# A fixed order for three layer norms: scale and shift of a channel chunk one step ahead, and later places for the transpositions of the later chunks

## The chip, the cores and the metric

The kernel runs on one core of a Trainium2 chip. The metric is the device time of one execution, in microseconds (us). Its engines work side by side and each takes its instructions in the order written for it: TensorE (PE, with its weight loads shown apart as PEld), VectorE (DVE), ScalarE (ACT), GpSimd (POOL), and SyncE (SP), which issues the transfers.

## The reference

Two decoder layers over 256 positions of 2048 channels. What matters here is the frame around the mixers:

```python
for layer in range(DEPTH):                       # DEPTH = 2
    mix = even_mixer(...) if layer % 2 == 0 else odd_mixer(...)
    h = layer_norm(DEEPNORM_ALPHA * h + mix, ln_g[layer, 0], ln_b[layer, 0])
    ffn = conv_ffn(h, ffn_w_up[layer], ...)      # (silu(conv(x@up_a)) * (x@up_u)) @ w_down
    h = layer_norm(DEEPNORM_ALPHA * h + ffn, ln_g[layer, 1], ln_b[layer, 1])
```

So there are four layer norms. Each ends a matrix product whose result it needs whole (mean and variance run over all 2048 channels), and the product that follows each of the first three needs its output. All is float32.

## The kernel before, in words

**Products.** A float32 number is split into a high part `hi` and a rest `lo`, both in a format that TensorE multiplies, and a product is made of three: hi with hi, hi with lo, lo with hi. Weights come from memory in slabs: SP issues the load of a slab into one of four buffers `wraw` (L102), ACT writes `whi` (L108), DVE writes `wlo` (L109), each again into one of four buffers. The call that does these three for the next slab is named "pump". Nearly all of the kernel is a stream of such slabs with matmuls behind it.

**What sets the order.** The products are emitted one after another; a scheduler that knows the dependencies sets the order on the engines. Between the two marks `strict_from` and `strict_to`, which lie around each norm, every engine but SP keeps exactly the order in which the program wrote its instructions. SP's transfers are placed by the scheduler.

**A norm.** Tokens come in two halves, t = 0 and t = 1, of 128 each, on the partitions; `r` holds the 2048 channels as four chunks c = 0 to 3 of 512. For the last column group of the product before the norm, the matmuls of half 0 end first and those of half 1 are held back (the stretch "t1"), to give the norm of half 0 something to hide behind. Then, for each half and chunk (two digits, "12" is half 1, chunk 2):

- `first` and `second` on DVE (L226, L230): subtract the mean and multiply by the gain, then multiply by the inverse deviation and add the bias. Both work on `r` in place; `shift` is the two of them. Gains and biases lie in tiles borrowed from the feed-forward part (`tmp`, `c`, `u`, `row`, `fpad`), by their chunk.
- `turn`: four transpositions of 128x128 on TensorE (L255) into a PSUM tile `ps`, then ACT copies them to the `hi` part of `x` (L256).
- `lo` on DVE (L261): the rest, into the `lo` part of `x`.

`x` holds 16 k-tiles (128 channels each), so a chunk is four of them.

**The head of the next product.** While the norm runs, TensorE starts on the next product with the k-tiles that are there already; the first weight slabs for it lie ready in a place of their own. In the norms 0 and 2 (the feed-forward product follows) the head has eight k-tiles and three passes, `h0` (half 0), `h1` (half 1) and `lo` (the lo parts of the weights), done in `head_b` (L341 and L348); its stream goes on in `group_b` (L317). In norm 1 (the odd mixer's input product follows) the head has four k-tiles and two passes `h0` and `h1`, done in `head_a`, and `group_a` goes on from k-tile 4 (places "on"); all its matmuls stand on L356 to L358. After each k-tile the program calls `turns.at(place, k)`, and the table `plan` of the class `Norm` says which steps are written there. Norm 3 ends the kernel and has no such table.

At the pumps of the table the slabs behind the head are prepared: slabs 8 to 11 in the norms 0 and 2, slabs 4 to 7 in norm 1.

Of the kernel before, what the change touches and what calls it, by code (L numbers as in the profile page):

```python
# [80 lines left out]
class Weights:  # L81


    def __init__(self, tc, pool, streams):
        self.tc, self.nc, self.pool, self.slabs, self.done = tc, tc.nc, pool, [], 0
        at = {k: 0 for k in streams}
        self.first = []
        for src, kind, parts, nk in jobs():
            width = sum(n for _, n in parts)
            self.first.append(len(self.slabs))  # L90
            for m in slab_sizes(kind, nk):
                self.slabs.append((streams[src], at[src], kind, m, width))
                at[src] += 128 * m * width
        self.ready = {}
        self.limit = len(self.slabs)
# [64 lines left out]
class Norm:  # L160


    def __init__(self, trunk, idx, stats):
        self.k, self.idx, self.stats = trunk, idx, stats
        small = trunk.small
        self.mv = small.tile([128, 2, 2], F32, name="mv", bufs=2)
        self.rs = small.tile([128, 2, 2], F32, name="rs", bufs=2)
        self.plan = {}
        if idx == 3:
            x = trunk.keep.tile([128, 2, DM], F32, name="x")  # L170
            self.gb = [[x[:, i, 512 * c:512 * c + 512] for i in range(2)] for c in range(4)]
        else:
            self.gb = trunk.row_tiles()
            p = "fill", 0, 0
            self.plan = {("t1", 5): ["turn00", "lo00"], ("t1", 7): ["turn01"], ("norm", 0): ["first00", "first01", "second00", "second01"],
                         ("norm", 1): ["lo01", "shift10", "shift11"]}
            if idx == 1:
                more = {("h0", 2): ["turn10", "lo10"], ("h1", 0): ["pump", "turn11", "lo11"],
                        ("h1", 1): ["pump", "shift02", "turn02", "lo02"],
                        ("h1", 2): ["pump", "shift12", "turn12", "lo12"],  # L180
                        ("h1", 3): ["shift03", "pump", "shift13"], ("on", 5): ["turn03", "lo03"],
                        ("on", 7): ["turn13", "lo13"]}
            else:
                more = {("h0", 5): ["turn10", "lo10"], ("h0", 7): ["turn11", "lo11"],
                        ("h1", 3): ["shift02", "turn02", "lo02", "pump"],
                        ("h1", 6): ["shift12", "turn12", "lo12", "pump"],
                        ("lo", 1): ["shift03", "turn03", "lo03", "pump"],
                        ("lo", 4): ["shift13", "turn13", "lo13", "pump"]}
            self.plan.update(more)
        gb = trunk.I["gb"]  # L190
        for c in range(4):
            for i in range(2):
                trunk.nc.sync.dma_start(self.gb[c][i], bass.AP(
                    tensor=gb.tensor, offset=gb.offset + 4096 * idx + 2048 * i + 512 * c, ap=[[0, 128], [1, 512]]))
        self.ps = {}
# [1074 lines left out]
```

## Time and profile before

| | |
|---|---|
| time, median of 3 runs | 2329.18 us (2328.76 to 2329.88) |
| the profiled execution's own time | 2331.47 us |
| its span, first to last instruction | 2329.7 us |
| mean granted TensorE clock over the span | 0.996 |
| busy: PE, DVE, ACT | 2300.9, 1420.1, 1105.4 us |
| norm 0, from its first turn to the end of its head | 376.5 to 406.4 us |
| norm 1, the same | 1119.1 to 1142.8 us |
| norm 2, the same | 1576.4 to 1604.9 us |

Times in a timeline count from the first instruction of the span. A row of the timeline gives start, duration, engine, line and operation, what it writes and reads, how often (rows that follow one another at once are merged), and in brackets the idle time of the engine before it with what ended it. Matmuls overlap, so the distance of two starts says more than a duration.

### The profile page before, as it was taken

The page shows a single profiled execution, that of the slowest core. Times are in us where ns is not written, and L with a number is a line of the kernel's source. Part 1 is how long each engine was busy: PE and PEld are TensorE (multiplying, and loading weights), DVE is VectorE, ACT ScalarE, POOL GpSimd, SP SyncE. Part 2 cuts the span into 40 slices and gives each one's busy share as a digit, 9 for nine tenths or more (in the row PEclk, how much of TensorE's full clock was granted, in tenths as well). Part 3 has the DMA queues.
Part 4 walks back from the last instruction along what each step waited for, and adds up shares of the span by engine and source line. Part 5 has one row for each costly group of instructions (what it writes and reads, how often), then busy time and mean ns, then how long its engine had stood idle before and what let it go on. Part 6 is the DMA issues. An engine that isn't in the chain of part 4 may idle for free.

```text
span 2329.7 us, 32013 instructions
## 1 busy us (share of the span) xinstructions
PE 2300.9 (99%) x12550; PEld 1986.0 (85%) x12550; DVE 1420.1 (61%) x1921; ACT 1105.4 (47%) x1429; POOL 20.5 (1%) x32
## 2 busy tenths in 40 slices
PE   9999999999999999999999999999999999999998
PEld 9888888888888888888789888888888888888886
DVE  5677666666666664445645667766666666654445
ACT  5554542555555554334345554444555555543332
POOL 0001000000000000000000000000000000000000
PEclk9999999999999999999999999999999999999999
DMA  8664474666666667667456734583666666676664
GB/s 284 192 192 148 161 239 126 192 189 189 185 190 189 190 197 215 196 192 224 146 165 213 222 104 140 164 275 108 192 190 186 188 190 188 189 223 198 194 191 143
DMA packets 128248, 436.63 MB, mean 187 GB/s; under 512 B 14256, under 2 KB 16992, under 8 KB 127712
## 3 DMA queue, kind: packets, MB, share of 16 engines
q1 hardware_dynamic: 128096, 434.58, 60.5%
q8 instruction: 98, 1.61, 0.3%
q14 instruction: 54, 0.44, 0.1%
HBM read 432.41 MB, written 2.11 MB: 187 GB/s over the span
## 4 chain that ended last, share of the span: by engine, by line
PE 96%; DVE 1%; DMA 1%; ACT 0%; issue 0%; SPq 0%; POOL 0%; DVEq 0%; ACTq 0%; POOLq 0%
PE acc L317 57%; PE acc L356 10%; PE acc L358 10%; PE acc L357 10%; PE ps L358 1%; PE ps L356 1%; PE ps L357 1%; PE ps L676 1%; DMA wraw<-in_ev_in 1%; PE ps L255 1%; DVE wlo L109 1%; PE acc L341 0%; PE ps L317 0%; PE ps L615 0%; ACT whi L108 0%; DVE r L230 0%
## 5 line engine op out<-in xcount | busy, mean ns | idle before, releaser
L109 DVE TENSOR_TENSOR wlo<-wraw,whi 128x1024 fp32r<-128x1024 f32 (+4 forms) x794 | 950.0, 1198 | 640.8 <-ACT whi L108 639.4
L317 PE MATMUL acc<-x,whi 128*128 128x512 f32 x3776 | 1178.3, 397 | 0.0
L108 ACT ACTIVATE whi<-wraw 128x1024 fp32r<-128x1024 f32 (+4 forms) x794 | 822.9, 1037 | 732.8 <-PE acc L358 290.2
L317 PEld LDWEIGHTS acc<-x,wlo 128*128 128x128 f32 x3776 | 692.4, 188 | 156.6 <-issue 0.2
L317 PE MATMUL acc<-x,wlo 128*128 128x256 f32 x3776 | 726.1, 279 | 0.0
L317 PEld LDWEIGHTS acc<-x,whi 128*128 128x128 f32 x3776 | 584.2, 189 | 12.5 <-issue 1.2
L356 PE MATMUL acc<-whi,A 128*128 128x512 f32 x448 | 175.9, 393 | 0.0
L358 PE MATMUL acc<-whi,A 128*128 128x512 f32 x448 | 174.5, 390 | 0.0
L357 PE MATMUL acc<-wlo,A 128*128 128x512 f32 x448 | 174.5, 390 | 0.0
L408 ACT ACTIVATE tmp<-acc 128x512 f32<-128x512 f32 x120 | 71.6, 597 | 215.9 <-PE acc L317 213.8
L356 PE MATMUL acc<-whi,B 128*128 128x512 f32 x388 | 150.9, 389 | 0.0
L357 PE MATMUL acc<-wlo,B 128*128 128x512 f32 x388 | 150.9, 389 | 0.0
L358 PE MATMUL acc<-whi,B 128*128 128x512 f32 x388 | 150.9, 389 | 0.0
L358 PEld LDWEIGHTS acc<-whi,A 128*128 128x128 f32 x448 | 84.1, 188 | 17.7 <-DVE A L277 0.3
L356 PEld LDWEIGHTS acc<-whi,A 128*128 128x128 f32 x448 | 84.1, 188 | 17.3 <-ACT A L276 0.4
L357 PEld LDWEIGHTS acc<-wlo,A 128*128 128x128 f32 x448 | 84.2, 188 | 17.0
L356 PE MATMUL acc<-whi,x 128*128 128x512 f32 (+4 forms) x272 | 93.3, 344 | 0.3 <-ACT V L697 0.3
L357 PE MATMUL acc<-wlo,x 128*128 128x512 f32 (+4 forms) x272 | 92.9, 342 | 0.0
L358 PE MATMUL acc<-whi,x 128*128 128x512 f32 (+4 forms) x272 | 92.8, 341 | 0.0
L356 PEld LDWEIGHTS acc<-whi,B 128*128 128x128 f32 x388 | 72.8, 188 | 15.2
L357 PEld LDWEIGHTS acc<-wlo,B 128*128 128x128 f32 x388 | 72.8, 188 | 15.1
L358 PEld LDWEIGHTS acc<-whi,B 128*128 128x128 f32 x388 | 72.8, 188 | 15.1
(289 smaller groups left out, 1630.6 us busy)
## 6 DMA issues: line engine op xcount, KB each, us to landing
wraw<-in_up SPq DMA_DIRECT2D x328, 512.0 KB, 3.9
wraw<-in_down SPq DMA_DIRECT2D x176, 512.0 KB, 4.2
wraw<-in_od_in SPq DMA_DIRECT2D x96, 512.0 KB, 4.1
wraw<-in_ev_in SPq DMA_DIRECT2D x72, 512.0 KB, 3.6
wraw<-in_ev_out SPq DMA_DIRECT2D x32, 512.0 KB, 4.1
wraw<-in_od_out SPq DMA_DIRECT2D x32, 512.0 KB, 4.4
wraw<-in_up SPq DMA_DIRECT2D x32, 384.0 KB, 3.5
wraw<-in_ev_in SPq DMA_DIRECT2D x16, 348.0 KB, 4.5
```

What stands on the lines that cost most here:

```text
L108: nc.scalar.activation(hi[:, :n], raw[:, :n], AF.Copy)
L109: nc.vector.tensor_tensor(lo[:, :n], raw[:, :n], hi[:, :n].bitcast(F32), op=OP.subtract)
L255: nc.tensor.transpose(ps[:, 128 * i:128 * i + 128], T.r[:, t, 512 * c + 128 * i:512 * c + 128 * i + 128], T.ident)
L317: nc.tensor.matmul(acc, wt, mv, start=(k == 0 and i < len(unit)), stop=(k == nk - 1 and i >= len(unit)))
L356: nc.tensor.matmul(o, xh, wh, start=first, stop=False)
L357: nc.tensor.matmul(o, xh, wl, start=False, stop=False)
L358: nc.tensor.matmul(o, xl, wh, start=False, stop=last)
L408: nc.scalar.activation(t, a[:, :, 256:], AF.Copy, scale=sign)
L676: nc.tensor.matmul(o[:, t * 128:(t + 1) * 128], a, b, start=(i == 0), stop=(i == len(mms) - 1))
```

## The change

Only the table `plan` is changed, for the norms 0 to 2. No instruction is added, taken away or altered. The lines behind the table stand three lines higher afterwards (L255 is L252, L226 is L223, L230 is L227, L261 is L258, L915 is L912).

```diff
             if idx == 1:
-                more = {("h0", 2): ["turn10", "lo10"], ("h1", 0): ["pump", "turn11", "lo11"],
-                        ("h1", 1): ["pump", "shift02", "turn02", "lo02"],
-                        ("h1", 2): ["pump", "shift12", "turn12", "lo12"],
-                        ("h1", 3): ["shift03", "pump", "shift13"], ("on", 5): ["turn03", "lo03"],
-                        ("on", 7): ["turn13", "lo13"]}
+                more = {("h0", 2): ["turn10", "lo10", "shift02"], ("h1", 0): ["turn11", "lo11", "shift12", "pump"],
+                        ("h1", 1): ["turn02", "lo02", "shift03", "pump"],
+                        ("h1", 2): ["turn12", "lo12", "shift13", "pump"], ("h1", 3): ["pump"],
+                        ("on", 5): ["turn03", "lo03"], ("on", 7): ["turn13", "lo13"]}
             else:
-                more = {("h0", 5): ["turn10", "lo10"], ("h0", 7): ["turn11", "lo11"],
-                        ("h1", 3): ["shift02", "turn02", "lo02", "pump"],
-                        ("h1", 6): ["shift12", "turn12", "lo12", "pump"],
-                        ("lo", 1): ["shift03", "turn03", "lo03", "pump"],
-                        ("lo", 4): ["shift13", "turn13", "lo13", "pump"]}
+                more = {("h0", 5): ["turn10", "lo10"], ("h0", 7): ["turn11", "lo11", "shift02", "shift12"],
+                        ("h1", 4): ["turn02", "lo02", "pump"], ("h1", 7): ["turn12", "shift03", "lo12", "pump"],
+                        ("lo", 3): ["turn03", "shift13", "lo03", "pump"], ("lo", 6): ["turn13", "lo13", "pump"]}
```

DVE in norm 0, from the step lo10 on, before. L261 is `lo`, L226 and L230 are `first` and `second` (tile `u` and `row`: chunk 2; `fpad`: chunk 3), L109 is the DVE part of a pump.

```order
L261 TENSOR_TENSOR x<-ps,x 128x4x128 x2
L226 SCALAR_TENSOR_TENSOR r<-r,mv,u 128x512
L230 SCALAR_TENSOR_TENSOR r<-r,rs,row 128x512
L261 TENSOR_TENSOR x<-ps,x 128x4x128
L109 TENSOR_TENSOR wlo<-wraw,whi 128x768
L226 SCALAR_TENSOR_TENSOR r<-r,mv,u 128x512
L230 SCALAR_TENSOR_TENSOR r<-r,rs,row 128x512
L261 TENSOR_TENSOR x<-ps,x 128x4x128
L109 TENSOR_TENSOR wlo<-wraw,whi 128x768
L226 SCALAR_TENSOR_TENSOR r<-r,mv,fpad_3392 128x512
L230 SCALAR_TENSOR_TENSOR r<-r,rs,fpad_3393 128x512
```

The same place after the change:

```order
L258 TENSOR_TENSOR x<-ps,x 128x4x128 x2
L223 SCALAR_TENSOR_TENSOR r<-r,mv,u 128x512
L227 SCALAR_TENSOR_TENSOR r<-r,rs,row 128x512
L223 SCALAR_TENSOR_TENSOR r<-r,mv,u 128x512
L227 SCALAR_TENSOR_TENSOR r<-r,rs,row 128x512
L258 TENSOR_TENSOR x<-ps,x 128x4x128
L109 TENSOR_TENSOR wlo<-wraw,whi 128x768
L223 SCALAR_TENSOR_TENSOR r<-r,mv,fpad_3392 128x512
L227 SCALAR_TENSOR_TENSOR r<-r,rs,fpad_3393 128x512
L258 TENSOR_TENSOR x<-ps,x 128x4x128
L109 TENSOR_TENSOR wlo<-wraw,whi 128x768
```

The scale and shift of 12 now stands ahead of the `lo` of 02 and its pump, and that of 03 ahead of the `lo` of 12. Norm 2 has the same rows.

DVE in norm 1, from lo10 on, before. `A<-prm` writes a small piece for the odd mixer into the area `A`, which holds the head's weight slabs until TensorE is done with them.

```order
L261 TENSOR_TENSOR x<-ps,x 128x4x128
L109 TENSOR_TENSOR wlo<-wraw,whi 128x1024
L261 TENSOR_TENSOR x<-ps,x 128x4x128
L109 TENSOR_TENSOR wlo<-wraw,whi 128x1024
L226 SCALAR_TENSOR_TENSOR r<-r,mv,u 128x512
L230 SCALAR_TENSOR_TENSOR r<-r,rs,row 128x512
L261 TENSOR_TENSOR x<-ps,x 128x4x128
L109 TENSOR_TENSOR wlo<-wraw,whi 128x1024
L226 SCALAR_TENSOR_TENSOR r<-r,mv,u 128x512
L230 SCALAR_TENSOR_TENSOR r<-r,rs,row 128x512
L261 TENSOR_TENSOR x<-ps,x 128x4x128
L226 SCALAR_TENSOR_TENSOR r<-r,mv,fpad_9188 128x512
```

The same place after the change, down to the last `second`:

```order
L223 SCALAR_TENSOR_TENSOR r<-r,mv,u 128x512
L227 SCALAR_TENSOR_TENSOR r<-r,rs,row 128x512
L109 TENSOR_TENSOR wlo<-wraw,whi 128x1024
L258 TENSOR_TENSOR x<-ps,x 128x4x128
L223 SCALAR_TENSOR_TENSOR r<-r,mv,fpad_9188 128x512
L227 SCALAR_TENSOR_TENSOR r<-r,rs,fpad_9189 128x512
L109 TENSOR_TENSOR wlo<-wraw,whi 128x1024
L258 TENSOR_TENSOR x<-ps,x 128x4x128
L223 SCALAR_TENSOR_TENSOR r<-r,mv,fpad_9188 128x512
L274 TENSOR_TENSOR A<-prm,A 128x16x2 x2
L227 SCALAR_TENSOR_TENSOR r<-r,rs,fpad_9189 128x512
L109 TENSOR_TENSOR wlo<-wraw,whi 128x1024 x3
```

The `shift` of 02 has gone ahead of lo11 (it stands above the first of these rows), that of 12 ahead of the first pump; each pump comes one step later, and the wlo of the slabs 6 and 7 stand behind the last `shift`.

SP in norm 1, before and then after: slabs 4 to 11 of the odd input product, the small loads `row` and `cs` for the odd mixer, further slabs, `dec` (1 MB).

```order
L102 DMA wraw<-in_od_in 128x1024 x8
L915 DMA row<-in_c_row 128x1
L967 DMA cs<-in_c_rot 128x512
L102 DMA wraw<-in_od_in 128x1024
L968 DMA dec<-in_c_decay 128x2048
L102 DMA wraw<-in_od_in 128x1024 x19
```

```order
L102 DMA wraw<-in_od_in 128x1024 x6
L912 DMA row<-in_c_row 128x1
L964 DMA cs<-in_c_rot 128x512
L102 DMA wraw<-in_od_in 128x1024 x5
L965 DMA dec<-in_c_decay 128x2048
L102 DMA wraw<-in_od_in 128x1024 x17
```

The loads `row` and `cs` are issued two slabs earlier, ahead of the slabs 10 and 11, and `dec` two slabs later.

## The prediction

> **What bounds the kernel now.** I read the page's busy times first, then TensorE's own waits, then the timeline of the engines around each norm, and last the stretches with their granted clock.
>
> ```profile
> PE 2300.9 (99%) x12550; PEld 1986.0 (85%) x12550; DVE 1420.1 (61%) x1921; ACT 1105.4 (47%) x1429; POOL 20.5 (1%) x32
> PE ps L255 <- DVE r L230: 15.8, 8, 3.1
> PE ps L255 <- DVE r L230: 5.4, 3, 1.8
> PE ps L255 <- DVE r L230: 4.9, 2, 3.1
> ```
>
> TensorE is the bound, with DVE and ACT far behind. The waits (total us, times, longest) name one cause that matters: the transposition (L255) waits for `second` (L230), 15.8 us in eight waits, over half of the 2329.7 - 2300.9 = 28.8 us that TensorE is idle at all. The last two rows are the same question for the stretches of norm 0 and norm 1; norm 2 answers like norm 0. So all a better order can win is here, plus what a stop drags behind it. DVE in norm 0 shows why the shift is late:
>
> ```profile
> 386.24 0.69 DVE L261 TENSOR_TENSOR x<-ps,x 128x512 fp32r<-128x512 f32 x1 [1.17 <-ACT x L256]
> 386.85 0.74 DVE L226 SCALAR_TENSOR_TENSOR r<-r,mv,u 128x512 f32<-128x512 f32 x1
> 387.63 0.75 DVE L230 SCALAR_TENSOR_TENSOR r<-r,rs,row 128x512 f32<-128x512 f32 x1
> 389.82 0.69 DVE L261 TENSOR_TENSOR x<-ps,x 128x512 fp32r<-128x512 f32 x1 [1.44 <-ACT x L256]
> 390.55 0.96 DVE L109 TENSOR_TENSOR wlo<-wraw,whi 128x768 fp32r<-128x768 f32 x1
> 391.43 0.75 DVE L226 SCALAR_TENSOR_TENSOR r<-r,mv,u 128x512 f32<-128x512 f32 x1
> 392.21 0.75 DVE L230 SCALAR_TENSOR_TENSOR r<-r,rs,row 128x512 f32<-128x512 f32 x1
> 393.11 0.63 PE L255 MATMUL ps<-ident,r 128*128 128x128 f32 x4 [1.81 <-DVE r L230]
> ```
>
> After the shift of 02 (done at 388.38) DVE idles 1.44 us for lo02, which needs ACT's copy of turn02; lo02 and the pump come next, and only then the shift of 12, which was ready to run at 388.4. turn12 starts 0.15 us after its end (392.96), with TensorE 1.81 us idle. The shift is not slow; it stands in the wrong place.
>
> **The change part by part.** Nothing is added, so the sum is each norm's stretch now, less the same matmuls without gaps. First norm 0:
>
> ```profile
> 384.98 0.60 PE L255 MATMUL ps<-ident,r 128*128 128x128 f32 x4
> 385.33 0.48 PE L341 MATMUL acc<-x,B 128*128 128x256 f32 x2
> 387.09 0.40 PE L341 MATMUL ps<-x,B 128*128 128x256 f32 x2
> 387.81 0.40 PE L341 MATMUL ps<-x,B 128*128 128x256 f32 x2
> 388.05 0.40 PE L341 MATMUL acc<-x,B 128*128 128x256 f32 x2
> 389.19 0.60 ACT L256 ACTIVATE x<-ps 128x512 fp32r<-128x512 f32 x1 [2.98 <-PE ps L255]
> 406.42 0.63 PE L317 MATMUL acc<-x,whi 128*128 128x512 f32 x2
> 408.52 0.63 PE L317 MATMUL acc<-x,whi 128*128 128x512 f32 x2
> 1588.02 0.40 PE L341 MATMUL acc<-x,B 128*128 128x256 f32 x2
> 1604.87 0.63 PE L317 MATMUL acc<-x,whi 128*128 128x512 f32 x2
> ```
>
> A k-tile of the head takes 387.81 - 387.09 = 0.72 us, a turn 385.33 - 384.98 = 0.35. The fourth k-tile of `h1` ends at 388.05 + 0.24 = 388.29, and slab 8 (L317) starts at 406.42: 18.13 us for 12 k-tiles and 4 turns, which are worth 12 x 0.72 + 4 x 0.35 = 10.04. Norm 2: 1604.87 - 1588.26 = 16.61, for the same 10.04. So 8.09 and 6.57 us are there to be won.
>
> Does the new order wait anywhere? Times of norm 0, with the durations quoted. Shift 02 ends at 388.38, as now; shift 12 follows at once and ends at 389.9. turn02, one k-tile later, is due at 389.0: 0.5 us to spare over the 0.15. ACT's copy follows a turn's start by 0.66 (389.19, for turn02 at 388.53): 389.66 to 390.26; lo02 to 390.95, wlo of slab 8 to 391.95, shift 03 to 393.45. turn12 is due at 391.5 (shift ended 389.9), turn03 at 394.7 (393.45). lo12 to 394.15, wlo 9 to 395.1, shift 13 to 396.6; turn13 is due at 397.25, spare 0.5. Slab 8 is due at 398.3 and was ready at 391.95; slab 11 after lo13 at about 400.2, due three slabs of 408.52 - 406.42 = 2.1 us after slab 8, at 404.6. So no new wait: the full 8.09 and 6.57. Without this cover (a turn late by d) TensorE stops for d, no more.
>
> Norm 1 is the tight one:
>
> ```profile
> 1128.75 0.60 PE L255 MATMUL ps<-ident,r 128*128 128x128 f32 x4
> 1129.10 0.47 PE L356 MATMUL acc<-A,x 128*128 128x512 f32 x1
> 1130.10 0.39 PE L357 MATMUL acc<-A,x 128*128 128x512 f32 x1
> 1130.33 0.40 PE L358 MATMUL acc<-A,x 128*128 128x512 f32 x1
> 1133.78 1.09 PE L255 MATMUL ps<-ident,r 128*128 128x128 f32 x4 [3.05 <-DVE r L230]
> 1142.75 0.62 PE L356 MATMUL acc<-whi,x 128*128 128x512 f32 x1
> 1148.83 0.47 PE L356 MATMUL acc<-whi,x 128*128 128x512 f32 x1
> 1154.38 0.60 PE L255 MATMUL ps<-ident,r 128*128 128x128 f32 x4
> 1130.01 0.69 DVE L261 TENSOR_TENSOR x<-ps,x 128x512 fp32r<-128x512 f32 x1 [1.04 <-ACT x L256]
> 1130.96 1.23 DVE L109 TENSOR_TENSOR wlo<-wraw,whi 128x1024 fp32r<-128x1024 f32 x1 [0.26 <-ACT whi L108]
> 1132.10 0.75 DVE L226 SCALAR_TENSOR_TENSOR r<-r,mv,u 128x512 f32<-128x512 f32 x1
> 1143.26 0.32 DVE L277 TENSOR_TENSOR A<-prm,A 128x32 fp32r<-128x32 f32 x2 [0.85 <-ACT A L276]
> ```
>
> The second k-tile of `h1` ends at 1130.33 + 0.23 = 1130.56, and k-tile 4 starts at 1142.75: 12.19 us for two turns and two k-tiles of 1130.56 - 1129.10 = 1.46, or 2 x 0.35 + 2 x 1.46 = 3.62. To be won: 8.57.
>
> DVE from lo11 at 1130.01, now without a pause: shift 12 to 1132.2 (turn12 is due at 1132.37, with 0.15 for the signal: just in time), wlo 4 to 1133.45 (k-tile 4 due at 1134.18), lo02, shift 03 to 1135.7, wlo 5 to 1136.9 (due at 1136.9), lo12, `first` of 13, A<-prm, `second` to 1139.4, wlo 6 to 1140.6. k-tile 6 is due at 1134.18 + 5.55 + 0.35 = 1140.1 (5.55 is two k-tiles, 1154.38 - 1148.83), its product with wlo 0.23 later: late by 0.3. But the rows start closer than their durations (1130.96 to 1132.10 is 1.14 for a wlo of 1.23), and with those distances the wait is gone. Bounds 0 to 0.5; I take 0.2. What stands behind a late wlo 6 is wlo 7 (1141.9, due at 1142.8) and lo03, not due before k-tile 12.
>
> SP: `row` is waiting for the last `second` and now stands ahead of the slabs 10 and 11.
>
> ```profile
> 1146.07 0.75 DVE L230 SCALAR_TENSOR_TENSOR r<-r,rs,fpad 128x512 f32<-128x512 f32 x1
> 1146.90 0.33 SPq L915 DMA_DIRECT2D row<-in_c_row x1
> wraw<-in_od_in SPq DMA_DIRECT2D x96, 512.0 KB, 4.1
> ```
>
> It was issued at 1146.90, with `second` done at 1146.82; now at 1139.5. Slab 10 waits for wlo 6 (1140.6) anyhow, lands 4.1 later and then wants one ACT and one DVE operation (the latter 1.23): ready by 1147.5, due at 1151.5. Nothing. The same holds for the gain row that passes slab 12 in the norms 0 and 2: it waits for shift 12, which now ends earlier. `dec` moves by two slabs; its load has until the odd mixer's late part.
>
> **The clock.** Part of the sum is not idle time:
>
> ```profile
> 402.25:406.42 4.17, 4.14 (x22) 4.17 (x23) 1.65 (x2) 1.33 (x2) 0.04 (x1) 0.59 0.18 65
> 1602.25:1604.87 2.62, 2.62 (x23) 2.62 (x23) 1.29 (x2) 1.33 (x2) 0.01 (x1) 1.00 0.34 125
> 1130.56:1142.75 12.19, 7.27 (x22) 5.48 (x21) 7.47 (x10) 3.45 (x5) 0.00 (x0) 0.60 0.36 123
> ```
>
> The granted clock is the third last number. The end of norm 0's head ran at 0.59, norm 2's, with the same gaps, at 1.00: 4.17 - 2.62 = 1.55 us. In norm 1 the clock fell in the 3.05 gap: 12.19 - 3.62 - 4.9 of waits leaves 3.6, nearly all of it clock. I hold that gaps bring this on, and that it depends on when they fall; without gaps both go. The Trainium skill, "TensorE: Matmul & The Clock Gate", section "HAM oscillation — how this bites in real kernels", lets the clock fall only behind idle gaps of more than about 3.4 us. No gap here is that long, yet the clock falls in two of three norms, so the trace does not bear the figure out; by it the sum would be that of the first rival below.
>
> Sum, from the profiled execution: 8.09 + 6.57 + 8.57 - 0.2 = 23.0, so 2331.47 would be 2308.4. The timed runs lie 2.3 us lower (median 2329.18). If that is the recording, it is common to both; if the drop in norm 0 did not happen in them, 1.55 of the gain is not there to win. I take half of it: 22.2, so 2329.18 - 22.2 = 2307.0.
>
> **The rivals.**
>
> *The clock drops stay.* If they are not the gaps' doing, only idle time and restarts go: 23.0 - 1.55 - 3.6 = 17.9, 2311.3. Against it: the one norm without a drop shows the rest of the head at 1.00. Chance 0.06. (The Trainium skill's figure, taken strictly, leads here as well.)
>
> *DVE becomes the bound in norm 1.* Its row from 1130.0 to 1140.6 has no pause, and turn12, slab 5 and slab 6 are due within 0.3 us of being ready. Some more us per operation, or a signal later than 0.15, and the waits come back there; half of 8.57 lost is 2311.3, all of it 2315.6. For: no slack. Against: each wait can only be as long as DVE is late, and DVE has no other work then. Chance 0.10.
>
> *The change doesn't do what it says:* the turns wait for something else, say a free PSUM tile, and the releaser is misnamed; 2329, no change. Against: all long gaps end 0.15 us after a `second`, and lo02, which frees a tile, was done at 390.51, long before 393.11. Chance 0.05.
>
> *Slower: the pauses were paying for the clock.* A denser TensorE is granted less over the whole program. Each 0.01 of mean clock costs 0.01 x 2300.9 = 23 us, so from 0.986 in place of 0.996 on the gain is eaten, and 0.98 gives 2307 + 37 = 2344. For: the grant does change within one execution. Against: TensorE is busy for 99% of the span already, at a mean of 0.996. Chance 0.03.
>
> **How the numbers follow.** Forecast 0.76: 2307.0, its own range 2304.5 (a drop in norm 2 too, another 1.5, and no wait) to 2310. With the clock rival and the nearer half of the DVE rival the range is 2304.5 to 2313, some 0.85. Faster by over 0.2% (4.7 us, about what a measurement of this kernel tells from no change): 0.76 + 0.06 + 0.10 = 0.92. Same 0.05, slower 0.03.
>
> **What would show it.** In the changed profile, TensorE's waits should have no "PE ps L252 <- DVE r L227" over 1 us in total (now 15.8); from the fourth k-tile of `h1` to slab 8, 10 to 10.5 us in the norms 0 and 2; in norm 1 from turn02 to k-tile 4 3.6 to 4.1; granted clock 1.00 in all three; PE's new wait, if any, on wlo (L109) in norm 1. I am wrong if gaps of over 1 us stand behind another releaser, or if the span falls by less than 17.

## The result and the profile after

| | before | after |
|---|---|---|
| time, median of 4 runs | 2329.3 us (2328.76 to 2329.88) | 2309.46 us (2309.12 to 2310.49) |
| the profiled execution's own time | 2331.47 us | 2309.18 us |
| its span | 2329.7 us | 2307.4 us |

The ratio is 0.9916, with a 95% interval of 0.9898 to 0.9933: 19.8 us faster, forecast were 22.2 (2307.0, range 2304.5 to 2313).

TensorE's waits after the change (line and what it waited for; total us, times, longest):

```profile
PE ps L568 <- DMA wraw<-in_ev_in: 1.8, 1, 1.8
PE ps L1158 <- DVE pad L719: 1.1, 1, 1.1
PE acc L353 <- ACT V L694: 0.3, 1, 0.3
PE ps L1099 <- ACT gny L1092: 0.2, 1, 0.2
```

The wait of the transposition for `second`, 15.8 us in eight pieces before, is gone from the list; all that is left existed before (the first, at the start of the kernel, was 0.7 then). To put the three norms side by side I measure each from the start of turn11 to the first matmul behind the head. The stretches of the kernel before (us from to, length, busy times, and third from the end the granted clock), then those after:

```profile
384.98:406.42 21.44, 15.94 (x118) 15.24 (x117) 13.04 (x18) 5.92 (x9) 0.20 (x2) 0.92 0.22 68
1128.75:1142.75 14.00, 9.08 (x32) 6.85 (x30) 8.24 (x11) 4.63 (x6) 0.00 (x0) 0.65 0.35 113
1584.94:1604.87 19.93, 14.43 (x119) 13.74 (x117) 12.69 (x18) 5.93 (x9) 0.20 (x2) 1.00 0.20 61
```

```profile
385.44:399.13 13.69, 13.69 (x119) 13.69 (x118) 11.09 (x16) 5.12 (x9) 0.21 (x2) 1.00 0.30 78
1121.40:1126.88 5.48, 5.48 (x31) 4.60 (x30) 4.37 (x7) 4.28 (x6) 0.00 (x0) 1.00 0.01 1
1568.88:1582.57 13.69, 13.69 (x118) 13.69 (x117) 11.09 (x16) 5.11 (x9) 0.21 (x2) 1.00 0.21 61
```

After the change TensorE is busy for every microsecond of all three, at full clock. 7.75 + 8.52 + 6.24 = 22.5 us went there, and the two spans differ by 22.3. So the profile shows what the forecast's sum said (23.0), while the medians moved by less. Why, is the question of the experiments on the clock below.

How the order works now is seen on DVE and PE in norm 0 (times here are 0.46 us later than before, from the kernel's start):

```profile
388.09 0.75 DVE L227 SCALAR_TENSOR_TENSOR r<-r,rs,row 128x512 f32<-128x512 f32 x1
388.76 0.75 DVE L223 SCALAR_TENSOR_TENSOR r<-r,mv,u 128x512 f32<-128x512 f32 x1
389.54 0.75 DVE L227 SCALAR_TENSOR_TENSOR r<-r,rs,row 128x512 f32<-128x512 f32 x1
390.74 0.69 DVE L258 TENSOR_TENSOR x<-ps,x 128x512 fp32r<-128x512 f32 x1 [0.45 <-ACT x L253]
392.07 0.60 PE L252 MATMUL ps<-ident,r 128*128 128x128 f32 x4
```

The shift of 12 fills the time in which DVE used to idle for ACT's copy, and is done at 390.29; turn12 comes at 392.07 and waits for nothing. Norm 1, DVE first, then PE:

```profile
1124.06 0.75 DVE L227 SCALAR_TENSOR_TENSOR r<-r,rs,row 128x512 f32<-128x512 f32 x1
1124.72 1.22 DVE L109 TENSOR_TENSOR wlo<-wraw,whi 128x1024 fp32r<-128x1024 f32 x1
1127.90 1.22 DVE L109 TENSOR_TENSOR wlo<-wraw,whi 128x1024 fp32r<-128x1024 f32 x1
1131.17 3.49 DVE L109 TENSOR_TENSOR wlo<-wraw,whi 128x1024 fp32r<-128x1024 f32 x3
1125.05 0.60 PE L252 MATMUL ps<-ident,r 128*128 128x128 f32 x4
1126.88 0.39 PE L353 MATMUL acc<-whi,x 128*128 128x512 f32 x1
1132.69 0.47 PE L353 MATMUL acc<-whi,x 128*128 128x512 f32 x1
1133.01 0.39 PE L354 MATMUL acc<-wlo,x 128*128 128x512 f32 x1
```

The shift of 12 ends at 1124.81, its turn starts at 1125.05: 0.24 later, of which 0.15 is the signal. The wlo of slab 6 (the first of the three from 1131.17) ends near 1132.4 and is used at 1133.01.

### The profile page after: what moved, and what is told of

It is laid out like the page before. It is cut to its first block, busy times and chain, and to the rows that moved or that the text cites. A ratio compares the mean times of both kernels' runs of the same rounds, so it can differ in the third digit from the quotient of the medians.

```text
span 2307.4 us, 32010 instructions
## 1 busy us (share of the span) xinstructions
PE 2293.4 (99%) x12550; PEld 1981.4 (86%) x12550; DVE 1418.0 (61%) x1921; ACT 1105.0 (48%) x1429; POOL 21.6 (1%) x32
## 4 chain that ended last, share of the span: by engine, by line
PE 98%; DMA 1%; DVE 1%; ACT 0%; issue 0%; SPq 0%; POOL 0%; DVEq 0%; ACTq 0%; POOLq 0%
PE acc L314 57%; PE acc L353 10%; PE acc L355 10%; PE acc L354 10%; PE ps L353 1%; PE ps L354 1%; PE ps L355 1%; PE ps L673 1%; DMA wraw<-in_ev_in 1%; PE acc L338 1%; PE ps L314 0%; PE ps L252 0%; PE ps L612 0%; PE ps L639 0%; PE ps L338 0%; PE acc L345 0%
## 5 line engine op out<-in xcount | busy, mean ns | idle before, releaser
L109 DVE TENSOR_TENSOR wlo<-wraw,whi 128x1024 fp32r<-128x1024 f32 (+4 forms) x794 | 949.2, 1198 | 635.4 <-ACT whi L108 634.2
```

The costliest lines, as they stand in the source:

```text
L109: nc.vector.tensor_tensor(lo[:, :n], raw[:, :n], hi[:, :n].bitcast(F32), op=OP.subtract)
```

## The experiments

Two questions: which part of the table makes the gain, and why the medians gained 2.5 us less than the profiled spans. My theory is that the shift's place on DVE is the whole cause, that each norm's gain is its own, and that the clock falls because of the gaps. The rivals are that the later turns or the later pumps do it, and that the clock has other reasons.

### The new table in norms 0 and 2 alone, and in norm 1 alone

Of each table only the entries that differ are shown.

```diff
 # against the changed kernel. The run with norms 0 and 2:
-more = {("h0", 2): ["turn10", "lo10", "shift02"], ("h1", 0): ["turn11", "lo11", "shift12", "pump"],
-        ("h1", 1): ["turn02", "lo02", "shift03", "pump"],
-        ("h1", 2): ["turn12", "lo12", "shift13", "pump"], ("h1", 3): ["pump"],
+more = {("h0", 2): ["turn10", "lo10"], ("h1", 0): ["pump", "turn11", "lo11"],
+        ("h1", 1): ["pump", "shift02", "turn02", "lo02"],
+        ("h1", 2): ["pump", "shift12", "turn12", "lo12"], ("h1", 3): ["shift03", "pump", "shift13"],
 # the run with norm 1:
-("h0", 7): ["turn11", "lo11", "shift02", "shift12"],
-("h1", 4): ["turn02", "lo02", "pump"], ("h1", 7): ["turn12", "shift03", "lo12", "pump"],
-("lo", 3): ["turn03", "shift13", "lo03", "pump"], ("lo", 6): ["turn13", "lo13", "pump"]
+("h0", 7): ["turn11", "lo11"],
+("h1", 3): ["shift02", "turn02", "lo02", "pump"], ("h1", 6): ["shift12", "turn12", "lo12", "pump"],
+("lo", 1): ["shift03", "turn03", "lo03", "pump"], ("lo", 4): ["shift13", "turn13", "lo13", "pump"]
```

> The new table for norms 0 and 2 only; norm 1 keeps the old one. Theory (each norm's gain is its own: gaps and the clock that falls in them): no wait of a transposition in norms 0 and 2, two waits of 4.9 us in all in norm 1, and there the clock at about half again. By the two profiles norms 0 and 2 give 7.75 + 6.43 = 14.2 us, so 2329.3 - 14.2 = 2315.1; if the clock drop of norm 0 was peculiar to the profiled execution, 12.6, so 2316.7. Rival (the clock falls for another reason than the gaps): the low clock shows up in a norm without gaps, or not in norm 1 at all.

> The new table for norm 1 only; norms 0 and 2 keep the old one. Theory: no wait in norm 1, three waits of 1.8 us in each of norms 0 and 2, which may or may not bring the clock down. Gain 8.6 us (2320.7) if the timed runs of the kernel before have the clock drop in norm 1 as its profile has; 5.2 (2324.1) if they have not. With e1 it has to add up to the whole gain of 19.8. Rival (one norm's gain depends on the other's, through the transfers or the clock): the two don't add up within 1 us.

Measured: norms 0 and 2 alone (e1) 2317.35 us, ratio 0.9949 (0.9937 to 0.9962), a gain of 11.9 on the median before (2329.2 over 16 runs, 2327.71 to 2332.63); norm 1 alone (e2) 2321.98, ratio 0.9968 (0.9957 to 0.9980), a gain of 7.2. Together 19.1, against 19.8 for the whole: they add up within the microsecond allowed. Neither gain is one of the two that I had expected (14.2 or 12.6 for e1, 8.6 or 5.2 for e2): e1 lies below both, e2 between them. The trace of e1 has two waits in norm 1, 5.1 us in all. The stretches, norm 1 of e1 (old table there), then norms 0 and 2 of e2 (old table):

```profile
1120.93:1134.03 13.10, 8.00 (x32) 6.07 (x31) 8.14 (x11) 4.63 (x6) 0.00 (x0) 0.81 0.36 121
```

```profile
384.90:404.83 19.93, 14.42 (x119) 13.72 (x118) 12.69 (x18) 5.92 (x9) 0.20 (x2) 1.00 0.23 73
1574.56:1594.82 20.26, 15.95 (x118) 15.25 (x117) 12.65 (x18) 5.92 (x9) 0.20 (x2) 0.92 0.21 61
```

The norms with the new table took 13.68, 13.69 and 5.49 us, as in the whole change. Those with the old table differ from one execution to the next: norm 1 14.00 before and 13.10 here, norm 0 21.44 before and 19.93 here, norm 2 19.93 before and 20.26 here. The granted clock differs along with them.

### Shift one step ahead, turns at their old k-tiles (norms 0 and 2; norm 1 as changed; e3, against the changed kernel)

```diff
-("h1", 4): ["turn02", "lo02", "pump"], ("h1", 7): ["turn12", "shift03", "lo12", "pump"],
-("lo", 3): ["turn03", "shift13", "lo03", "pump"], ("lo", 6): ["turn13", "lo13", "pump"]
+("h1", 3): ["turn02", "lo02", "pump"], ("h1", 6): ["turn12", "shift03", "lo12", "pump"],
+("lo", 1): ["turn03", "shift13", "lo03", "pump"], ("lo", 4): ["turn13", "lo13", "pump"]
```

> Norm 1 as in the change; in norms 0 and 2 the scale and shift are one step ahead as in the change, but the transpositions stay at their old k-tiles. Theory (the place of the shift behind lo and pump is the whole cause): the shift of 12 ends at 389.9 where its turn is due at 391.1, that of 03 at 393.0 where it is due at 393.7, that of 13 at 396.0 for 396.3; only turn02 waits 0.25 us as before, so 0.5 us over the changed kernel at most: 2309.5 to 2310. Rival (the later places of the turns are needed): waits of 0.5 us and more at several turns, 2311 to 2314.

Measured: 2309.08 us, ratio to the kernel before 0.9916 (0.9903 to 0.9930), the same as the whole change, and a little under the expected 2309.5 to 2310. Its norms 0 and 2:

```profile
384.13:398.07 13.94, 13.86 (x118) 13.69 (x117) 12.29 (x18) 5.92 (x9) 0.21 (x2) 1.00 0.29 85
1567.86:1581.81 13.95, 13.87 (x119) 13.70 (x118) 12.29 (x18) 5.93 (x9) 0.21 (x2) 1.00 0.23 64
```

13.94 against 13.69: the 0.25 us of turn02 in each, as expected, too little to be seen in the times. The later places of the turns, the second half of what the change does, are not needed.

### Turns later, each shift still right ahead of its turn (norms 0 and 2; norm 1 as before; e4, against the kernel before)

```diff
-("h1", 3): ["shift02", "turn02", "lo02", "pump"], ("h1", 6): ["shift12", "turn12", "lo12", "pump"],
-("lo", 1): ["shift03", "turn03", "lo03", "pump"], ("lo", 4): ["shift13", "turn13", "lo13", "pump"]
+("h1", 4): ["shift02", "turn02", "lo02", "pump"], ("h1", 7): ["shift12", "turn12", "lo12", "pump"],
+("lo", 3): ["shift03", "turn03", "lo03", "pump"], ("lo", 6): ["shift13", "turn13", "lo13", "pump"]
```

> Norm 1 as before; in norms 0 and 2 the transpositions stand at the later k-tiles of the change, each with its scale and shift right ahead of it as before. Theory: the loop turn, copy, lo, pump, shift takes 4.58 us as before (393.11 - 388.53), against 3, 4 and 3 k-tiles of 0.72 and a turn of 0.43, so gaps of 2.0, 1.3 and 2.0 us stay in each of the two norms: 5.3 in place of 5.7, time 2328.5. Rival (it is the later place that hides the shift): the gaps go in norms 0 and 2, 2315 to 2317.

Measured: 2327.27 us, ratio 0.9992 (0.9984 to 1.0001), so not told from no change by its interval. The gaps in norm 0:

```profile
393.28 0.63 PE L255 MATMUL ps<-ident,r 128*128 128x128 f32 x4 [1.81 <-DVE r L230]
397.87 0.63 PE L255 MATMUL ps<-ident,r 128*128 128x128 f32 x4 [1.09 <-DVE r L230]
402.46 0.63 PE L255 MATMUL ps<-ident,r 128*128 128x128 f32 x4 [1.81 <-DVE r L230]
```

The turns still follow each other at 4.59 us, whatever k-tiles stand between: the loop over copy, lo, pump and shift sets the pace. One more k-tile takes 0.72 off one gap and turn02's 0.25 goes, so the stretch is 18.94 against 19.93. The theory's order of size held, but my 5.3 in place of 5.7 mixed two ways to count a gap: the trace shows 4.7 us of idle time in place of 5.5 (19.93 - 14.43), and a gap lengthens its stretch by some 0.18 us more than the trace shows it. That is seen best in norm 0 of the run with four extra operations (e6, below), which has one gap: shown as 1.24 us, while the stretch is 15.11 against 13.69, 1.42 longer.

```profile
393.05 0.63 PE L257 MATMUL ps<-ident,r 128*128 128x128 f32 x4 [1.24 <-DVE r L227]
385.02:400.13 15.11, 13.87 (x118) 13.70 (x117) 13.68 (x20) 5.11 (x9) 0.21 (x2) 1.00 0.23 70
```

### Norm 1: pumps back to the front, and pumps late without the shift ahead

```diff
 # against the changed kernel: pumps first (e8)
-("h1", 0): ["turn11", "lo11", "shift12", "pump"], ("h1", 1): ["turn02", "lo02", "shift03", "pump"],
-("h1", 2): ["turn12", "lo12", "shift13", "pump"],
+("h1", 0): ["pump", "turn11", "lo11", "shift12"], ("h1", 1): ["pump", "turn02", "lo02", "shift03"],
+("h1", 2): ["pump", "turn12", "lo12", "shift13"],
 # pumps late, shifts right ahead of their turns (e9)
-("h0", 2): ["turn10", "lo10", "shift02"], ("h1", 0): ["turn11", "lo11", "shift12", "pump"],
-("h1", 1): ["turn02", "lo02", "shift03", "pump"],
-("h1", 2): ["turn12", "lo12", "shift13", "pump"], ("h1", 3): ["pump"],
+("h0", 2): ["turn10", "lo10"], ("h1", 0): ["turn11", "lo11", "pump"],
+("h1", 1): ["shift02", "turn02", "lo02", "pump"],
+("h1", 2): ["shift12", "turn12", "lo12", "pump"], ("h1", 3): ["shift03", "shift13", "pump"],
```

> The changed kernel with the pumps of norm 1 back at the start of their steps as before; scale and shift stay one step ahead. From turn11 to k-tile 4 the change takes 5.48 us in norm 1, the kernel before 14.0. Theory (only the place of the shift matters): DVE does the same operations in another order between lo10 and the shift of 12, which ends at 1124.8 as in the change: 5.5 us, no wait. Rival (the later pumps are what makes room on DVE): a wait ahead of turn12 of about one wlo, 1.1 us, so 6.5 or more.

> The changed kernel with scale and shift of norm 1 back right ahead of their turns, and the pumps later as in the change. Theory: turn02 waits for lo11, a wlo and the shift (about 2.9 us), turn12 for copy, lo, wlo and shift after turn02 (about 2.9): 11 us and the clock's drop, 11 to 14 us in all as before. Rival (the later pumps do it): under 8 us.

Measured in one execution each (2309.20 and 2317.06 us), e8 and then e9:

```profile
1121.39:1126.88 5.49, 5.49 (x31) 4.61 (x30) 5.46 (x8) 4.28 (x6) 0.00 (x0) 1.00 0.29 97
```

```profile
1120.66:1133.91 13.25, 8.07 (x31) 6.17 (x30) 7.81 (x10) 5.12 (x7) 0.00 (x0) 0.80 0.23 80
```

With the shift ahead 5.49, as in the change; with the later pumps alone 13.25, as before. In norm 1 too it is the place of the shift that makes the gain; the pumps' places alone make none.

### How much room is left, and what a gap does to the clock

Extra operations on DVE that nobody reads, ahead of the shift of 12, in three doses, against the changed kernel (e5: six, two and six for norms 0, 1 and 2; e6: four each; e7: nine, eight and nine):

```diff
+    def slow(self, t, n):
+        g = self.gb[0]
+        for _ in range(10 * t + n):
+            self.k.nc.vector.scalar_tensor_tensor(g[0], g[0], self.mv[:, 0, 0:1], g[1], op0=OP.subtract, op1=OP.mult)
-("h1", 0): ["turn11", "lo11", "shift12", "pump"]             # norm 1
+("h1", 0): ["turn11", "lo11", "slow02", "shift12", "pump"]   # 02, 04, 08
-("h0", 7): ["turn11", "lo11", "shift02", "shift12"]          # norms 0 and 2
+("h0", 7): ["turn11", "lo11", "shift02", "slow06", "shift12"]  # 06, 04, 09
```

> The changed kernel with operations of 128x512 that nobody reads (0.75 to 0.78 us each) on DVE ahead of the scale and shift of 12: six in norm 0, two in norm 1, six in norm 2. In the trace of the change, turn12 has 1.63 us to spare in norms 0 and 2 (due 392.07, shift 390.29 and 0.15) and 0.09 in norm 1 (due 1125.05, shift 1124.81 and 0.15). Theory (DVE is at its limit in norm 1, loose in the others): one gap ahead of turn12 of 6 x 0.77 - 1.63 = 3.0 in norms 0 and 2 and of 2 x 0.77 - 0.09 = 1.45 in norm 1 (the row shows some 0.15 less, since the last matmul drains), and nothing else waits. Rival (there is slack in norm 1 after all): no gap there. Clock: a gap of 1.4 leaves it at 1.00; one of 3 brings it to half in most cases, for a multiple of 3.4 us, as in norm 1 before (from 1133.0 to 1143.2). Rival on the clock: it has nothing to do with gaps, and falls where none is.

> As the run with 6, 2 and 6 such operations, with four in each norm. One gap ahead of turn12 of 4 x 0.77 - 1.63 = 1.45 us in norms 0 and 2 (clock stays at 1.00) and of 4 x 0.77 - 0.09 = 3.0 in norm 1 (clock falls to half, unless the gap is split evenly between two stretches of the 3.4 us grid). Rival on the clock: no relation to the gap's length.

> The same with nine operations in norms 0 and 2 and eight in norm 1: one gap ahead of turn12 of 9 x 0.77 - 1.63 = 5.3 us and of 8 x 0.77 - 0.09 = 6.1. Theory: the clock falls to half in all three norms, since such a gap always fills more than half of one stretch of 3.4 us, and comes back after one such stretch with matmuls. Rival: it stays at 1.00 in at least one of them.

turn12 in the run with six, two and six, norms 0, 1, 2; in the run with four, norm 1; and in the run with eight, norm 1:

```profile
394.74 0.63 PE L257 MATMUL ps<-ident,r 128*128 128x128 f32 x4 [2.81 <-DVE r L227]
1130.58 0.63 PE L257 MATMUL ps<-ident,r 128*128 128x128 f32 x4 [1.18 <-DVE r L227]
1584.07 1.09 PE L257 MATMUL ps<-ident,r 128*128 128x128 f32 x4 [2.81 <-DVE r L227]
```

```profile
1128.95 0.74 PE L257 MATMUL ps<-ident,r 128*128 128x128 f32 x4 [2.75 <-DVE r L227]
```

```profile
1139.80 1.09 PE L257 MATMUL ps<-ident,r 128*128 128x128 f32 x4 [5.92 <-DVE r L227]
```

Room: two operations cost norm 1 6.85 - 5.48 = 1.37 us of their 1.5, so some 0.1 us was free there, while six in norm 0 opened a gap of only 2.81. DVE is at its limit in norm 1 and loose in the other two. All these gaps came within 0.15 us of what I had expected. With eight, one more wait of 0.5 us for a wlo appeared; I had expected none. The three took 2320.41 (e5), 2316.31 (e6) and 2333.09 us (e7), one execution each.

Clock, over the three norms of all eleven profiles:

| gaps in a norm, us of idle PE as the rows show it | norms seen | clock fell in |
|---|---|---|
| none over 0.1 | 14 | 0 |
| one of 1.2 | 3 | 0 |
| two of 1.8 and one more of 0.6 to 1.8 | 6 | 2 |
| one of 2.8 | 3 | 3 |
| one of 3.05 and one of 1.9 to 2.3 | 4 | 4 |
| one of 5.2 to 5.9 | 3 | 3 |

So in the norms gaps bring the clock down, and it never fell without one. Elsewhere, apart from the end of the kernel, where TensorE runs out of work, it fell once: in the profile with nine, eight and nine, behind a gap of 1.23 us near the start of the kernel and two small matmuls (32 rows by 8 columns) after it; a gap of 1.78 us at the same place in the changed kernel did not bring it down. So a gap's length alone does not decide. The matmul behind that gap, and the 3.41 us at whose end the clock fell (its mean from 38.00 to 38.50 is 0.57):

```profile
36.82 0.80 PE L573 MATMUL ps<-oh,prm 32*8 32x384 f32 x2 [1.23 <-DMA wraw<-in_ev_in]
34.66:38.07 3.41, 2.18 (x11) 1.28 (x11) 0.41 (x1) 0.65 (x1) 0.00 (x0) 1.00 0.83 299
```

When the clock falls is not set by the gap's start either. Half microseconds of the kernel before, in norm 0 and norm 1:

```profile
402.50:403.00 0.50, 0.50 (x5) 0.50 (x4) 0.00 (x0) 0.00 (x0) 0.00 (x0) 0.55 0.86 332
405.50:406.00 0.50, 0.50 (x4) 0.50 (x4) 0.00 (x0) 0.00 (x0) 0.00 (x0) 0.54 0.00 0
1133.00:1133.50 0.50, 0.00 (x0) 0.00 (x0) 0.50 (x1) 0.00 (x0) 0.00 (x0) 0.50 0.63 106
1143.00:1143.50 0.50, 0.50 (x3) 0.36 (x3) 0.24 (x3) 0.35 (x2) 0.00 (x0) 0.76 0.00 0
```

A mean of 0.55 over a half microsecond puts the fall at 402.55 (a tenth of it at full clock), 0.54 the return at 405.96, the next fall at 1133.0, 0.76 its return at 1143.24. The distances are 3.41, 727.04 = 213 x 3.413, and 3 x 3.41. In e5 and e7, where it fell in several norms, falls and returns lie on such a grid too. The grid's place against the program is another in each execution, so how long a gap's slow clock lasts, and for the shorter gaps whether it comes at all, differs between executions of one program: norm 1 with the old table took 14.00, 13.10 and 13.25 us in three executions (before, e1, e4), and 13.25 with the late pumps of e9; norms 0 and 2 21.44, 19.93, 19.93 and 20.26.

Take 19.93 for norms 0 and 2, which was seen twice, and 13.25 for norm 1, seen once with the old table and once with the late pumps: 53.1 us, against 32.9 with the new one, is 20.2, and the medians moved by 19.8 and (e3) 20.1. The choice matters: with the means of all that was seen with the old table (20.39 and 13.45) it would be 21.4. The profiled execution before had 1.5 more in norm 0 and 0.75 more in norm 1, 2.3 in all, which is just what its time lay above the median (2331.47 against 2329.18). The timed runs of the kernel before have no trace, so that this was the difference in them is an inference from the sizes, not seen. What speaks for it is the mean granted clock, which each timed run has on record: of the 16 runs of the kernel before, the six at 0.996 took 2330.6 us on average, the ten at 0.997 or 0.998 2328.8. So its runs do get longer as the clock is lower, by a size near the one asked for (1.8 against 2.3 us); in which norm the clock fell in them stays open.

## Why the prediction was right, step by step

- **The bound and the cause** (the shift stands behind lo and pump): right. Shift ahead alone gives all of it in norms 0 and 2 (e3), pumps alone nothing in norm 1 (e9), turns alone 1 us in a stretch (e4). That the turns' new places matter was never claimed; e3 shows that they were not needed.
- **The sum of norms 0 and 2** (8.09 and 6.57): 7.75 and 6.24 in the profiles. The mis-sized term is the turn, taken at 0.35 us from its start to the next matmul's start. The rows after it show 0.08 more:

```profile
385.44 0.60 PE L252 MATMUL ps<-ident,r 128*128 128x128 f32 x4
385.79 0.48 PE L338 MATMUL acc<-x,B 128*128 128x256 f32 x2
386.11 0.40 PE L338 MATMUL ps<-x,B 128*128 128x256 f32 x2
```

  The pair of matmuls behind a turn takes 0.32 where a pair takes 0.24; four turns make 0.33 for each of the two norms. A turn costs 0.43.
- **Norm 1** (8.57, less 0.2 for a wait on slab 6): 8.52, and no wait. The wlo that I added up at 1.23 each come 1.14 apart, which the prediction named as the case without a wait. That turn12 would be just in time was right (0.1 us, e5).
- **The transfers** (nothing): right for TensorE. The load `row`, ahead of the slabs 10 and 11 now, went out at 1131.33, right behind the last `second`. One ACT operation waited for a slab of the sooner stream (1.53 us), and no matmul waited for it:

```profile
1131.33 0.33 SPq L912 DMA_DIRECT2D row<-in_c_row x1
1136.05 1.06 ACT L108 ACTIVATE whi<-wraw 128x1024 fp32r<-128x1024 f32 x1 [1.53 <-DMA wraw<-in_od_in]
```

- **The clock** (gaps bring it on, and both drops go): right, 14 norms without gaps show none. By the figure that I quoted from the Trainium skill ("TensorE: Matmul & The Clock Gate", "HAM oscillation — how this bites in real kernels"), only gaps over 3.4 us would do it; here single gaps of 2.8 did it three times in three. A late turn also costs more than the prediction's "TensorE stops for d, no more": the gap shown as 1.24 us in e6 cost 1.42, and those of 2.8 us or more half clock besides.
- **From the profile to the median** (subtract 22.2): this is the step that was too large, by 2.4 us. I took norm 1's drop in full and half of norm 0's as what a timed run holds. In the profiled execution both norms were longer than in most others; with stretches of 13.25 and 19.93 the same sum is 20.2, though that the timed runs had these is inferred. The other reading that I offered, that the recording costs a constant 2.3 us, does not hold: the changed kernel's profiled execution has 2309.18 where its timed runs have 2309.12 to 2310.49.
- **The rivals**: the clock drops did not stay; DVE in norm 1 is at its limit, but on the right side of it; the releaser was named rightly; no loss of clock over the whole span (mean 0.998 after, 0.996 before).

## What to carry to other kernels

In an order written by hand, an engine runs a ready operation only when the one ahead of it is done (here DVE's shift of 12 was ready at 388.4 and began at 391.43). So look for the operation ahead that waits for another engine, and write ready work that someone will wait for into that idle time. Before moving both ends of a wait, move the producer alone; here the consumer's new places were worth a quarter of a microsecond in each of two norms. A gap of TensorE cost its length as the trace shows it, some 0.2 us more, and, when some 1.8 us or more of one step of the grid was idle, at times half clock for one to three such steps of 3.4 us. So one profiled execution can overstate what the removal of a gap brings.

## What the runs showed of the hardware that I had not expected

The clock falls and returns on a free-running grid of 3.413 us: 402.55, 405.96, 1133.00 and 1143.24 in one execution lie 1, 213 and 3 steps apart. It fell behind single gaps of 2.8 us (three of three) and behind rows of 1.8 us gaps twice in six.

The idle time within one step of the grid sorts the cases better than the length of a gap. With the steps laid from each profile's own falls and returns, and counting the steps up to the end of norm 2 that began at full clock: each of the 12 with 1.9 us or more of idle TensorE had the clock fall at its end, of the 8 with 1.80 or 1.81 two did, and of those with less only the one of 1.23 with the small matmuls. In the kernel before, a gap of 1.81 that lay whole within a step (395.89 to 397.70) did not bring the clock down, and one in the next step (400.47 to 402.28) did; the shortest idle time of the 12 was in norm 2 of the run with six, two and six (the last row, 3.41 - 1.49).

```profile
395.72:399.14 3.42, 1.61 (x15) 1.47 (x14) 1.94 (x4) 0.78 (x2) 0.00 (x0) 1.00 0.41 121
399.14:402.55 3.41, 1.60 (x15) 1.43 (x14) 2.92 (x4) 0.56 (x1) 0.20 (x2) 1.00 0.22 68
1579.77:1583.18 3.41, 1.49 (x13) 1.28 (x11) 3.27 (x6) 0.70 (x1) 0.00 (x0) 1.00 0.00 0
```

At the end of the kernel, where TensorE runs out of work, it is the same: the clock fell behind the 7 steps that had 2.1 us or more of idle time, and not behind the 4 that had 1.89 or less. What decides at 1.8 us stays open.
